# Output projection of a hybrid encoder layer: token tiles fetched at the same place, scaled, cast and split five pieces later

## The chip, the cores and the metric

The kernel runs on one core of a Trainium2 chip. The metric is the device time of one execution in microseconds (us), and the time of a kernel is the median of its runs. Engines are named as in the profile: PE is the matrix engine and PEld its weight loads, DVE the vector engine, ACT the scalar engine, POOL the GpSimd engine, and SP the engine whose queue (SPq) issues the DMAs. "PEclk" is the clock that PE was granted, as a share of full speed.

## What is computed

One encoder layer over 2048 tokens of width 1024, in float32. Two mixers run on one input projection, a chunked state-space mixer (SSD) and an RWKV-7 mixer, each bidirectional and 512 wide; an output projection, a residual with layer norm, and an MLP follow.

```
y_ssd = ssd_bidir(z, xbc, dt_raw, ...)                  # (2048, 512), RMS-normed in two groups, times norm_g
y_rwkv = rwkv7_bidir(rw, mu_rwkv, ...)                  # (2048, 512)
mix = concatenate([y_ssd, y_rwkv], -1) @ w_out          # the output projection, (2048, 1024)
h = layer_norm(ALPHA * h + mix, ln1_g, ln1_b)
h = layer_norm(ALPHA * h + square(relu(h @ w_fc)) @ w_proj, ln2_g, ln2_b)
```

## The kernel before

The program has three stages. `phase_in` makes the input projection and starts the SSD; `phase_rwkv` runs the RWKV recurrence and, in its gaps, what is left of the SSD and then the output projection; `phase_mlp` takes up what remains of the output projection and runs the MLP. In the profile the recurrence runs from about 1060 to 1970 us.

**The recurrence.** `phase_rwkv` walks over 32 units `u` (16 chunks of tokens, two groups of heads). A unit has four generators that `weave` interleaves: `chain(u)`, the serial part, whose state passes through `zt` (L1182), `zv` (L1185) and PE's products `ch` (L1150); `prep(u + 3)`, which loads `rk`, `bk0` and `E` (L997 to L1001) and makes the operands `bk` (L1007), `kr` (L1009, L1024), `at` (L1025) and `ra` (L1026); `inverse(u + 2)`, which inverts 16x16 blocks on POOL in 15 steps of two instructions, `ltmp` and `ln` (L1065, L1066); and `merge(u + 1)`, which makes the 64x64 inverses of it. The inverse is reached through DRAM: `prep` writes `at` to `ad` (L1050), `inverse` reads it back as `la` (L1056), writes its result to `nd` (L1069) and reads that as `ni` (L1072). All these DMAs are issued by SP, one behind the other.

**The output projection.** `out_pieces` is a generator that is drawn on by `dense` at set points of `chain` and `merge`, eight pieces in a unit. A piece (`DENSE`) is three matmuls of 128x512; `HELD` ends a draw without work. Its first pass goes over the 16 token tiles with the SSD half of `w_out` (`products(ops, True)`: two halves of 512 columns, 12 matmuls each), the second pass with the RWKV half, from unit 19 on (`FA`), and ends in the layer norm.

**A token tile.** `load` (L813) fetches `h`, the residual (L815), `yr`, the mixer's output, in two DMAs (L818), and in the first pass `rsb`, the rows of RMS factors (L821). It then scales `yr` in four DVE instructions (L823), casts it to `yh` on ACT (L825) and takes the rest `yl` on POOL (L827). It is called one tile ahead, before the pieces of the tile in hand. The pool `part_w` has two buffers of each name, so the `yr` of tile j + 2 cannot be fetched before the `yl` of tile j has been taken.

**What sets the order.** The order in the code is the order of priority; a scheduler with a timeline of its own then places the instructions on each engine. On the chip an engine takes its instructions in that fixed order, and a waiting one holds all behind it.

Of the kernel before, what the change touches and what calls it, by code (L numbers as in the profile page):

```python
# [19 lines left out]
NT = T // P  # L20
# [182 lines left out]
def ppc(k, name, j):  # L203
    c = _PP[name] + j
    return k.pp[:, c:c + 1]
# [576 lines left out]
DENSE, HELD, LAST, END = "dense", "held", "last", object()  # L782


def out_pieces(k):
# [3 lines left out]
    with ExitStack() as ctx:  # L789
# [3 lines left out]
        def weights(c0):  # L793
            wh, wl = [cp.tile([P, 4, D], F32R, name=n) for n in ("woh", "wol")]

            def raw(i):
                w = wk.tile([P, 4, P], F32, name="yr").rearrange("p a t -> p (a t)")
                r = (c0 + i // 2) * P
                nc.sync.dma_start(w, I["w_out"][r:r + P, 512 * (i % 2):512 * (i % 2) + 512])
                return w  # L800

            w = raw(0)
            yield
            for i in range(8):
                nxt = raw(i + 1) if i < 7 else None
                cs = wh[:, i // 2, 512 * (i % 2):512 * (i % 2) + 512], wl[:, i // 2, 512 * (i % 2):512 * (i % 2) + 512]
                nc.scalar.copy(cs[0], w)
                nc.gpsimd.tensor_tensor(cs[1], w, cs[0], ALU.subtract)
                w = nxt
                yield  # L810
            k.wo = wh, wl

        def load(t, ys, first):  # L813
            h = wk.tile([P, D], F32, name="h")
            nc.sync.dma_start(h, k.hD[t])  # L815
            yr = wk.tile([P, 4, P], F32, name="yr")
            for g in range(2):
                nc.sync.dma_start(yr[:, 2 * g:2 * g + 2], ys[g][:, :, P * t:P * t + P].rearrange("a p t -> p a t"))  # L818
            if first:
                rsb = wk.tile([P, 2, P], F32, name="rsb")  # L820
                nc.sync.dma_start(rsb, rsD[:, t].unsqueeze(0).broadcast_to([P, 2, P]))  # L821
                for c in range(4):
                    nc.vector.scalar_tensor_tensor(yr[:, c], yr[:, c], ppc(k, "ng", c), rsb[:, c // 2], ALU.mult, ALU.mult)  # L823
            yh = wk.tile([P, 4, P], F32R, name="yh")
            nc.scalar.copy(yh, yr)  # L825
            yl = wk.tile([P, 4, P], F32R, name="yl")
            nc.gpsimd.tensor_tensor(yl, yr, yh, ALU.subtract)  # L827
            return t, h, yh, yl

        def products(ops, first, rows=None):  # L830
            (wh, wl), (t, h, yh, yl) = k.wo, ops
            for hf in range(2):
                hs = slice(512 * hf, 512 * hf + 512)
                pt = k.psg.tile([P, 512], F32, name=k.psg_name)
                mm = [(yh, wh), (yh, wl), (yl, wh)]
                mm = [(y[:, c], w[:, c, hs]) for c in range(4) for y, w in mm]
                for i, (y, w) in enumerate(mm):
                    nc.tensor.matmul(pt, y, w, start=(i == 0), stop=(i == 11))
                    if i == 11:
                        if first:  # L840
                            nc.vector.scalar_tensor_tensor(h[:, hs], h[:, hs], ALPHA, pt, ALU.mult, ALU.add)
                        else:
                            nc.vector.tensor_tensor(h[:, hs], h[:, hs], pt, ALU.add)
                    if i + 1 in (CUTS[2 * (t % 2) + hf] if first else (3, 6, 9, 12)):
                        yield DENSE
            if rows:
                ln_apply(k, wk, h, *rows, k.eps[:, 0:1], True)
            nc.sync.dma_start(k.hD[t], h)
# [42 lines left out]
        nc.sync.dma_start(rsD.rearrange("g c t -> (g c) t"), rt)  # L891
        yield
        order = [t for s in range(NT // 2, NT) for t in (NT - 1 - s, s)]
        ops = load(order[0], k.yS, True)
        for j in range(NT):
            nxt = load(order[j + 1], k.yS, True) if j + 1 < NT else None
            yield
            yield from products(ops, True)
            ops = nxt
        ws = weights(4)  # L900
        next(ws)
        for p in gates((0, 3)):
# [4 lines left out]
        rows = []  # L907
# [8 lines left out]
        nxt = None  # L916
        ready = lambda j: j < NT and k.final[order[j]] == 2
        for j in range(NT):
            while not ready(j):
                yield HELD  # L920
            if nxt:
                ops = nxt
            else:
                ops = load(order[j], k.yR, False)
                for _ in range(HL):
                    yield HELD
            while k.u < FA + j // FB:
                yield HELD
            nxt = load(order[j + 1], k.yR, False) if ready(j + 1) else None
            yield  # L930
            yield from products(ops, False, rows)
            k.finals = j + 1
            yield LAST


def phase_rwkv(k):
    nc, tc, I = k.nc, k.tc, k.I
    with ExitStack() as ctx:
# [321 lines left out]
        def weave(main, others):  # L1260
# [10 lines left out]
            for o in others:  # L1271
                if o[0] is not k.ssd:
                    while step(o[0], o[5]) is not END:
                        pass

        k.fill = out_pieces(k)
        k.credit = 0.0
        k.final = [0] * NT
# [23 lines left out]
def ln_apply(k, pool, x, g, b, eps, spread=False):  # L1302

    nc = k.nc
    mean, rs = ln_stats(k, pool, x, eps)
    if spread:
        sh = pool.tile([P, 1], F32, name="ln_sh")
        nc.vector.scalar_tensor_tensor(sh, mean, -1.0, rs, ALU.mult, ALU.mult)
        nc.scalar.activation(x, x, AF.Identity, scale=rs, bias=sh)
    for row, mul in ((g, True), (b, False)):  # L1310
        c = 0
        for r in row:
            cs = slice(c, c + r.shape[1])
            c = cs.stop
            if spread:
                nc.gpsimd.tensor_tensor(x[:, cs], x[:, cs], r, ALU.mult if mul else ALU.add)  # L1316
            elif mul:
                nc.vector.scalar_tensor_tensor(x[:, cs], x[:, cs], mean, r, ALU.subtract, ALU.mult)
            else:
                nc.vector.scalar_tensor_tensor(x[:, cs], x[:, cs], rs, r, ALU.mult, ALU.add)  # L1320
# [364 lines left out]
```

## Time and profile before

| | |
|---|---|
| median of 3 runs | 3360.61 us (3358.46 to 3367.17) |
| the profiled execution's own time | 3365.71 us |
| its span, first to last instruction | 3363.9 us |
| PE busy over the span | 2999.4 us (89%) |
| DVE, ACT, POOL busy | 2166.7, 1535.1, 1584.2 us |
| mean granted clock of PE | 0.92 |
| scaling of `yr` (L823) | x64, median 351 ns, 1147.5 to 1463.7 us |
| cast to `yh` (L825) | x32, median 618 ns |
| rest `yl` (L827) | x32, median 1280 ns |

A row of the timeline has the start, the length, the engine, the line, what is written from what, and how many instructions are merged into the row; in brackets how long the engine had been idle before it and what ended that. A row of windows has, for one stretch of time, the busy time of PE, PEld, DVE, ACT and POOL, the granted clock, the share of the DMA engines and the GB/s. A row of waits has the engine and line that waited, for what, the total, the number of times and the longest.

### The profile page before, as it was taken

What the parts mean: (1) busy time and instruction counts of PE and PEld (TensorE: products, weight loads), DVE (VectorE), ACT (ScalarE), POOL (GpSimd) and SP (SyncE); (2) the same over time, 40 slices, a digit from 0 to 9 for tenths busy, and PEclk for the clock granted to TensorE, in tenths of its full rate; (3) what the DMA queues carried; (4) which work ended last, traced back from release to release, by engine and by line L of the source; (5) the groups of instructions that cost most, each with busy time, mean ns of one, the idle gap of its engine ahead of it and who ended that gap; (6) DMA issues with size and microseconds to landing.
All of it is one profiled execution on the core that took longest, in us unless ns stands there. A gap on an engine that the chain in (4) does not pass through costs nothing. (4 is left out here: it accounts for less than half of the span.)

```text
span 3363.9 us, 63959 instructions
## 1 busy us (share of the span) xinstructions
PE 2999.4 (89%) x23783; PEld 2394.6 (71%) x23783; DVE 2166.7 (64%) x3671; ACT 1535.1 (46%) x2993; POOL 1584.2 (47%) x1972
## 2 busy tenths in 40 slices
PE   5979999988887799898898886999899989999997
PEld 3767877766675577676666664888787868887886
DVE  7798556667666455554577658767877744466446
ACT  3556323333334445455565544544544553344333
POOL 0352124444445333334466665555566335555645
PEclk9989999889886688897798887999999989999998
DMA  6445355776778666666666554777799475566554
GB/s 209 135 157 185 120 148 176 199 214 195 201 205 251 150 165 161 155 167 163 170 181 174 142 155 152 234 252 234 258 323 314 141 297 190 198 213 212 189 197 153
DMA packets 728183, 650.23 MB, mean 193 GB/s; under 512 B 204064, under 2 KB 578496, under 8 KB 727232
## 3 DMA queue, kind: packets, MB, share of 16 engines
q1 hardware_dynamic: 727872, 646.15, 62.5%
q8 instruction: 187, 3.06, 0.4%
q14 instruction: 124, 1.02, 0.1%
HBM read 403.43 MB, written 242.57 MB: 192 GB/s over the span
## 5 line engine op out<-in xcount | busy, mean ns | idle before, releaser
L1553 DVE TENSOR_TENSOR ul<-ul,uh 128x1024 fp32r<-128x1024 f32 x112 | 241.3, 2156 | 293.9 <-ACT uh L1552 293.6
L1553 POOL TENSOR_TENSOR pl<-pl,ph 128x1024 fp32r<-128x1024 f32 x112 | 287.9, 2575 | 277.9 <-ACT ph L1552 277.8
L1507 PE MATMUL ps<-hh,wh 128*128 128x512 f32 x896 | 352.2, 394 | 19.8 <-ACT wh L1370 6.6
L266 PE MATMUL psg<-hh,wh 128*128 128x512 f32 x864 | 357.2, 414 | 7.3 <-ACT u L285 6.6
L1611 PE MATMUL ps<-ph,uh 128*128 128x512 f32 x896 | 349.0, 392 | 10.4 <-ACT ph L1552 8.7
L1611 PE MATMUL ps<-pl,uh 128*128 128x512 f32 x896 | 351.6, 393 | 5.0 <-POOL pl L1553 5.0
L267 PE MATMUL psg<-hh,wl 128*128 128x512 f32 x864 | 354.5, 410 | 0.0
L268 PE MATMUL psg<-hl,wh 128*128 128x512 f32 x864 | 353.2, 410 | 1.4 <-DVE hl L236 1.4
L1507 PE MATMUL ps<-hl,wh 128*128 128x512 f32 x896 | 350.6, 392 | 1.5 <-DVE hl L1430 1.4
L1507 PE MATMUL ps<-hh,wl 128*128 128x512 f32 x896 | 351.0, 392 | 0.9 <-DVE wl L1371 0.9
L1611 PE MATMUL ps<-ph,ul 128*128 128x512 f32 x896 | 350.4, 392 | 0.0
L1371 DVE TENSOR_TENSOR wl<-wa,wh 128x512 fp32r<-128x512 f32 x217 | 209.5, 970 | 88.9 <-ACT wh L1370 87.9
L1065 POOL TENSOR_TENSOR ltmp<-ln,la 128x30 f32<-128x30 f32 (+10 forms) x480 | 123.6, 258 | 255.7 <-DMA la<-ad 225.6
L1552 ACT CAST ph<-pl 128x1024 fp32r<-128x1024 f32 x112 | 117.7, 1051 | 274.2 <-DMA pl<-pD 274.2
L1370 ACT CAST wh<-wa 128x512 fp32r<-128x512 f32 x217 | 133.0, 618 | 207.2 <-POOL wa L1343 100.2
L1507 PEld LDWEIGHTS ps<-hh,wh 128*128 128x128 f32 x896 | 169.8, 190 | 59.2 <-ACT wh L1370 7.9
L266 PEld LDWEIGHTS psg<-hh,wh 128*128 128x128 f32 x864 | 169.6, 196 | 47.4 <-ACT u L285 8.1
L1611 PEld LDWEIGHTS ps<-ph,uh 128*128 128x128 f32 x896 | 169.4, 189 | 47.0 <-ACT ph L1552 9.5
L1611 PEld LDWEIGHTS ps<-pl,uh 128*128 128x128 f32 x896 | 169.8, 190 | 43.9 <-POOL pl L1553 8.7
L268 PEld LDWEIGHTS psg<-hl,wh 128*128 128x128 f32 x864 | 168.4, 195 | 39.7 <-issue 3.4
L1507 PEld LDWEIGHTS ps<-hl,wh 128*128 128x128 f32 x896 | 169.5, 189 | 37.5 <-DVE hl L1430 1.8
L267 PEld LDWEIGHTS psg<-hh,wl 128*128 128x128 f32 x864 | 169.7, 196 | 36.3 <-issue 2.6
(322 smaller groups left out, 7087.6 us busy)
## 6 DMA issues: line engine op xcount, KB each, us to landing
uD<-ua SPq DMA_DIRECT2D x224, 256.0 KB, 2.9
ul<-uD SPq DMA_DIRECT2D x112, 512.0 KB, 4.6
pl<-pD SPq DMA_DIRECT2D x112, 512.0 KB, 3.7
wa<-in_w_fc_dram SPq DMA_DIRECT2D x124, 256.0 KB, 3.4
pD<-sc SPq DMA_DIRECT2D x112, 256.0 KB, 4.2
rk<-rk SPq DMA_DIRECT2D x64, 384.0 KB, 4.7
h<-hD SPq DMA_DIRECT2D x48, 512.0 KB, 4.0
eD<-et SPq DMA_DIRECT2D x32, 514.0 KB, 2.7
```

The source lines that it names most:

```text
L266: nc.tensor.matmul(pt, wh[:, c], hh[:, c], start=(c == 0), stop=False)
L267: nc.tensor.matmul(pt, wl[:, c], hh[:, c], start=False, stop=False)
L268: k.lag = nc.tensor.matmul(pt, wh[:, c], hl[:, c], start=False, stop=(c == KC - 1))
L1065: eng.tensor_tensor(tv, ln[:, 0:m, r:r + 1].broadcast_to([P, m, w]), la[:, r:r + 1, r + 1:16].broadcast_to([P, m, w]), ALU.mult)
L1370: nc.scalar.copy(hi, x)
L1371: nc.vector.tensor_tensor(lo, x, hi, ALU.subtract)
L1507: nc.tensor.matmul(pt, x, y, start=(n == 0 and i not in (2, 3)), stop=(n == 11 and i not in (1, 5)), skip_group_check=True)
L1552: nc.scalar.copy(hi, x)
L1553: eng.tensor_tensor(lo, x, hi, ALU.subtract)
L1611: nc.tensor.matmul(banks[j], x, z, start=(g == 0 and s == 0), stop=(g == NG - 1 and s == 5))
```

## The change

`load` is cut in two. `fetch` issues the DMAs of a tile and stands where `load` stood; `prepare` scales, casts and splits the tile. A new generator `after` passes the pieces of `products` on and calls `prepare` for the next tile once the sixth piece (number 5, counted from 0) has been made. For the very first tile `prepare` comes after four `HELD`, with one more behind it. In the second pass a tile that could not be fetched ahead is prepared after the `HL` draws that it already waited for.

```
-        def load(t, ys, first):
+        def fetch(t, ys, first):
             h = wk.tile([P, D], F32, name="h")
             nc.sync.dma_start(h, k.hD[t])
             yr = wk.tile([P, 4, P], F32, name="yr")
...
             if first:
                 rsb = wk.tile([P, 2, P], F32, name="rsb")
                 nc.sync.dma_start(rsb, rsD[:, t].unsqueeze(0).broadcast_to([P, 2, P]))
+                return t, h, yr, rsb
+            return t, h, yr, None
+
+        def prepare(raw):
+
+            t, h, yr, rsb = raw
+            if rsb is not None:
                 for c in range(4):
                     nc.vector.scalar_tensor_tensor(yr[:, c], yr[:, c], ppc(k, "ng", c), rsb[:, c // 2], ALU.mult, ALU.mult)
             yh = wk.tile([P, 4, P], F32R, name="yh")
...
-        ops = load(order[0], k.yS, True)
+        def after(pieces, raw, n=5):
+
+            ops = None
+            for i, p in enumerate(pieces):
+                if p is DENSE:
+                    if i == n and raw:
+                        ops = prepare(raw)
+                    yield p
+            return ops
+
+        raw = fetch(order[0], k.yS, True)
+        for _ in range(4):
+            yield HELD
+        ops = prepare(raw)
+        yield HELD
         for j in range(NT):
-            nxt = load(order[j + 1], k.yS, True) if j + 1 < NT else None
+            raw = fetch(order[j + 1], k.yS, True) if j + 1 < NT else None
             yield
-            yield from products(ops, True)
-            ops = nxt
+            ops = yield from after(products(ops, True), raw)
...
-                ops = load(order[j], k.yR, False)
+                raw = fetch(order[j], k.yR, False)
                 for _ in range(HL):
                     yield HELD
+                ops = prepare(raw)
             while k.u < FA + j // FB:
                 yield HELD
-            nxt = load(order[j + 1], k.yR, False) if ready(j + 1) else None
+            raw = fetch(order[j + 1], k.yR, False) if ready(j + 1) else None
             yield
-            yield from products(ops, False, rows)
+            nxt = yield from after(products(ops, False, rows), raw)
```

No instruction is added or taken away; the order on the engines changes from about 1147 us to the start of the MLP. Lines behind L821 have higher numbers in the changed kernel: L1182 (`zt`) becomes L1203, L1024 (`kr`) L1045, L827 (`yl`) L834, L1069 (`nd`) L1090.

On DVE, at the end of a unit of the first pass, before (`n` is a step of `merge`, `zt` and `zv` the state of the chain, `bk`, `kr` and `ra` operands of `prep`):

```order
L1024 TENSOR_TENSOR kr<-ps,rc 64x4x64 x2
L1097 STREAM_TRANSPOSE n_12093<-dd 128x256
L823 SCALAR_TENSOR_TENSOR yr<-yr,pp,rsb 128x128 x4
L1182 TENSOR_TENSOR zt<-zz_11640,ch 128x256
L1185 TENSOR_TENSOR zv<-zt,dtab 64x4x64 x2
L1186 TENSOR_TENSOR zz_11850<-zt,dtab 128x256
L841 SCALAR_TENSOR_TENSOR h<-h,psg 128x512
L1026 TENSOR_TENSOR ra<-ps,rc 128x4x64 x2
L1007 TENSOR_TENSOR bk<-bk_12306,E 128x2x128 x2
L1024 TENSOR_TENSOR kr<-ps,rc 64x4x64 x2
```

The same place in the changed kernel:

```order
L1118 STREAM_TRANSPOSE n_12075<-dd 128x256
L848 SCALAR_TENSOR_TENSOR h<-h,psg 128x512
L1203 TENSOR_TENSOR zt<-zz_11621,ch 128x256
L1206 TENSOR_TENSOR zv<-zt,dtab 64x4x64 x2
L1207 TENSOR_TENSOR zz_11832<-zt,dtab 128x256
L1047 TENSOR_TENSOR ra<-ps,rc 128x4x64 x2
L1028 TENSOR_TENSOR bk<-bk_12288,E 128x2x128 x2
L830 SCALAR_TENSOR_TENSOR yr<-yr,pp,rsb 128x128 x4
L1045 TENSOR_TENSOR kr<-ps,rc 64x4x64 x2
L1047 TENSOR_TENSOR ra<-ps,rc 128x4x64 x2
L1190 COPY zv<-ch 64x4x64
```

The four scalings have moved from right ahead of `zt` to behind `zt`, `zv` and the first `bk` of the next unit, right ahead of `kr`.

On POOL, in one inverse of the first pass, before (steps of `ltmp` and `ln`; the inverse starts with the 128x15 one):

```order
L1065 TENSOR_TENSOR ltmp<-ln,la 128x15
L1066 TENSOR_TENSOR ln<-ln,ltmp 128x15
L1065 TENSOR_TENSOR ltmp<-ln,la 128x14
L1066 TENSOR_TENSOR ln<-ln,ltmp 128x14
L1065 TENSOR_TENSOR ltmp<-ln,la 128x26
L1066 TENSOR_TENSOR ln<-ln,ltmp 128x2x13
L827 TENSOR_TENSOR yl<-yr,yh 128x512
L1065 TENSOR_TENSOR ltmp<-ln,la 128x24
```

The same inverse in the changed kernel, near its end (128x8 is the last step):

```order
L1086 TENSOR_TENSOR ltmp<-ln,la 128x21
L1087 TENSOR_TENSOR ln<-ln,ltmp 128x7x3
L834 TENSOR_TENSOR yl<-yr,yh 128x512
L1086 TENSOR_TENSOR ltmp<-ln,la 128x14
L1087 TENSOR_TENSOR ln<-ln,ltmp 128x7x2
L1086 TENSOR_TENSOR ltmp<-ln,la 128x8
L1087 TENSOR_TENSOR ln<-ln,ltmp 128x8
```

The rest `yl` has moved from behind the third step to behind the thirteenth of fifteen.

On SP, from the store of a finished tile to the read of the next `la`, before:

```order
L848 DMA hD_90<-h 128x1024
L818 DMA yr<-yS_128 128x2x128
L818 DMA yr<-yS_129 128x2x128
L815 DMA h<-hD_91 128x1024
L821 DMA rsb<-rsD 128x2x128
L1069 DMA nd<-ln 512x1x16
L1203 DMA yaD_125<-ye 128x2x128 x2
L1069 DMA nd<-ln 512x1x16
L999 DMA bk_12306<-bk_106 128x4x128
L997 DMA rk<-rk_105 128x6x128
L1072 DMA ni<-nd 64x8x16 x2
L1050 DMA ad<-at 64x8x64 x2
```

The same stretch in the changed kernel:

```order
L855 DMA hD_90<-h 128x1024
L818 DMA yr<-yS_128 128x2x128
L818 DMA yr<-yS_129 128x2x128
L1090 DMA nd<-ln 512x1x16
L815 DMA h<-hD_91 128x1024
L1224 DMA yaD_125<-ye 128x2x128 x2
L1090 DMA nd<-ln 512x1x16
L1018 DMA rk<-rk_105 128x6x128
L1020 DMA bk_12288<-bk_106 128x4x128
L821 DMA rsb<-rsD 128x2x128
L1093 DMA ni<-nd 64x8x16
L1071 DMA ad<-at 64x8x64 x2
```

The fetches of `h` and `rsb` now stand between the writes of `nd` and the write of `ad`, and one of the two reads of `ni` stands behind `ad`. The units of the changed kernel take turns in threes: in the next one `yaD` and `h` stand ahead of both `nd`, and in the one after that both `ni` stand ahead of `ad`.

## The prediction

> **What bounds the kernel now.** The change moves instructions only while the recurrence runs with the first and second pass of the output projection in its gaps. The chain of what ended last does not reach back into that stage (it begins at 2377.91 us), so I read the stage from windows cut at `zt`, the chain's state, which comes once a unit. The first window holds eleven units of the first pass; the three after it are single units in which the scaling of a tile no longer stands on DVE ahead of `zt`, as all 16 tiles are scaled by 1463.7 us.
>
> ```profile
> 1182.16:1463.98 281.82, 256.93 (x4708) 199.19 (x4708) 158.99 (x397) 137.97 (x396) 97.59 (x345) 0.88 0.63 163
> 1463.98:1483.60 19.62, 18.65 (x379) 14.52 (x379) 13.19 (x33) 11.17 (x33) 2.98 (x12) 1.00 0.54 122
> 1483.60:1509.00 25.40, 22.47 (x434) 17.75 (x430) 14.22 (x32) 12.44 (x36) 9.47 (x33) 0.93 0.62 162
> 1509.00:1536.60 27.60, 23.92 (x434) 18.61 (x429) 14.22 (x33) 12.43 (x36) 9.45 (x33) 0.88 0.53 142
> ```
>
> A unit takes 281.82 / 11 = 25.62 us. Next I read who waits in the eleven units.
>
> ```profile
> POOL ltmp L1065 <- DMA la<-ad: 105.8, 11, 10.9
> ...
> DVE yr L823 <- DMA yr<-yS: 36.2, 11, 6.0
> ...
> PE ch L1150 <- DVE zt L1182: 22.7, 10, 4.0
> ```
>
> So DVE sits 36.2 us before the scalings, in eleven waits, with `zt` right behind them, and PE then waits 22.7 us for `zt`. That is the stall at which the change is aimed. But POOL waits longer, once a unit, for `la`. Whether the first stall costs anything is a question of which loop closes last, so I followed one unit through POOL and SP.
>
> ```profile
> 1251.37 0.21 POOL L1065 TENSOR_TENSOR ltmp<-ln,la 128x15 f32<-128x15 f32 x1 [9.43 <-DMA la<-ad]
> ...
> 1253.05 1.27 POOL L827 TENSOR_TENSOR yl<-yr,yh 128x512 fp32r<-128x512 f32 x1
> ...
> 1260.42 0.33 POOL L1066 TENSOR_TENSOR ln<-ln,ltmp 128x21 f32<-128x21 f32 x1
> ...
> 1261.97 0.21 POOL L1066 TENSOR_TENSOR ln<-ln,ltmp 128x8 f32<-128x8 f32 x1
> ...
> 1276.51 0.31 POOL L1065 TENSOR_TENSOR ltmp<-ln,la 128x15 f32<-128x15 f32 x1 [8.65 <-DMA la<-ad]
> ```
>
> The inverse starts at 1251.37 (I call this point P), ends at 1262.18, and the next one starts at 1276.51: 25.14 us from P to P. What lies between is SP's queue:
>
> ```profile
> 1254.35 0.87 SPq L818 DMA_DIRECT2D yr<-yS  x2
> 1256.82 0.33 SPq L815 DMA_DIRECT2D h<-hD  x1
> 1259.90 0.36 SPq L821 DMA_DIRECT2D rsb<-rsD  x1
> 1262.21 0.55 SPq L1069 DMA_DIRECT2D nd<-ln  x1
> 1262.85 1.09 SPq L1203 DMA_DIRECT2D yaD<-ye  x2
> ...
> 1267.51 1.29 SPq L1072 DMA_DIRECT2D ni<-nd  x2
> 1268.85 1.64 SPq L1050 DMA_DIRECT2D ad<-at  x2
> 1270.74 0.42 SPq L999 DMA_DIRECT2D bk<-bk  x1
> 1272.59 1.67 SPq L1056 DMA_DIRECT2D la<-ad  x2
> ```
>
> `nd` leaves 0.03 us after the inverse ends; `ad`, of the next inverse, stands behind `ni` and leaves the moment `ni` has been issued; `la` follows when `ad` has landed. **Loop one** is thus 10.84 (P to `nd`) + 6.64 (`nd` to `ad`) + 3.74 (`ad` to `la`) + 3.92 (`la` to P) = 25.14 us. No scaling is in it. The rows of DVE and ACT close **loop two**:
>
> ```profile
> 1258.64 1.23 DVE L823 SCALAR_TENSOR_TENSOR yr<-yr,pp,rsb 128x128 f32<-128x128 f32 x4 [5.93 <-DMA yr<-yS]
> 1259.80 0.41 DVE L1182 TENSOR_TENSOR zt<-zz,ch 128x256 f32<-128x256 f32 x1
> ...
> 1266.51 0.88 DVE L1024 TENSOR_TENSOR kr<-ps,rc 64x256 f32<-64x256 f32 x2 [3.04 <-PE ps L1019]
> ```
>
> ```profile
> 1266.97 0.87 ACT L1025 COPY at<-ps 64x256 f32<-64x256 f32 x2 [1.35 <-DVE kr L1024]
> ```
>
> `yl` ends at 1254.32, and 0.03 us later SP sends for `yr`, whose buffer it frees; the scaling starts 4.32 us after `yl` ended, then come `zt`, `kr` and `at`, which is ready at 1267.84. That is 16.47 us after P, and SP reaches `ad` only at 17.48. So loop two has 1.0 us of slack: the stall is real and almost free. The three single units say the same. The first, 19.62 us, shows the chain running ahead once; the next two take 25.40 and 27.60 us without any scaling, since another wait has come in:
>
> ```profile
> 1501.50 0.76 DVE L1009 TENSOR_TENSOR kr<-rk,E 128x256 f32<-128x256 f32 x2 [3.93 <-DMA rk<-rk]
> ```
>
> `rk` is fetched by the same SP queue.
>
> **The change part by part.** No instruction is new; the four scalings, the cast and the split cost what they cost. Three things move.
>
> (a) *DVE.* The scalings leave the place ahead of `zt` for the one ahead of `kr`. What is late next there is again their `yr`. `zt` came 8.43 us after P (1259.80 - 1251.37); without 1.16 us of scaling, and with about 3.7 us from `zt` to the end of the first `bk`, DVE reaches the scalings at about P + 10.9. Queued behind them are `kr`, `ra` and the copy of `zv` for which PE's next chain product waits.
>
> (b) *POOL.* `yl` goes from behind step 3 to behind step 13. Step 13 ended at 1260.75 with one `yl` already done, so `yl` now ends at P + 9.38 rather than P + 2.95, and `yr` is sent for 6.4 us later. With the same 4.32 us it lands at P + 13.7: **the wait does not go, it is 2.8 us in place of 5.93 and stands one step later.** The unknown here is the landing under the new neighbours on the queue; the profile's median for these DMAs is the nearest row:
>
> ```profile
> yr<-yS SPq DMA_DIRECT2D x22, 128.0 KB, 3.8
> ```
>
> I keep 4.32, which holds the issue of both DMAs, with 3.8 below it and the longest wait of the table, 6.0, above. Then loop two becomes 9.38 + 4.32 + 1.16 (scaling) + 1.33 (`kr` start to `at` end, 1266.51 to 1267.84) = 16.19 us from P to `at`, against 16.47 before: the same length. At the lower bound it is 15.7, at the upper 17.9, which is 0.4 over the 17.48 at which SP is ready.
>
> (c) *SP.* Between `nd` and `ad` the units take turns in threes. In the first kind `h` (0.33) and `rsb` (0.36) come in and one `ni` (half of 1.29) goes behind `ad`: +0.04. In the second kind `yaD` (1.09) and `h` go ahead of `nd` and are issued while POOL still works: -1.09 + 0.36 - 0.65 = -1.38. In the third, `h` and `rsb` come in: +0.69. The mean is -0.22 us a unit, 12 units: **-2.6 us**. The bounds are all units like the second kind (-16.6) and all like the third (+8.3). In the second kind SP reaches `ad` at 17.48 - 1.38 = P + 16.1 and `at` is ready at 16.19, so nothing more can be won there.
>
> (d) *PE* has its gap elsewhere: in mid-unit, at the product behind the copy of `zv`, not at the unit's start. After a gap PE is slow for long:
>
> ```profile
> 1207.99 0.80 PE L838 MATMUL psg<-woh,yh 128*128 128x512 f32 x1
> ...
> 1225.98 0.39 PE L838 MATMUL psg<-wol,yh 128*128 128x512 f32 x1
> ```
>
> ```profile
> 1208.20:1236.30 28.10, 28.10 (x429) 21.84 (x430) 14.91 (x37) 12.61 (x37) 11.11 (x40) 0.68 0.57 147
> ```
>
> The same matmul costs 0.80 us at 1207.99 and 0.39 us only 18 us later, and the unit behind it has PE busy for 28.10 of 28.10 us at a granted clock of 0.68, where the first single unit above had 18.65 of 19.62 at 1.00. So a slow unit is one that PE itself bounds; I take the number of such units as unchanged, and leave the other case to the rivals.
>
> One rule speaks against such a price. The Trainium skill, page "TensorE: Matmul & The Clock Gate", Part 1 (The HAM clock gate), says that half clock comes after an idle window of about 3.4 us and full clock after some 3.4 us of sustained work. By it the second rival below has no price: an estimate from that page is 1.7 us lost for each gap, far from filling a unit, and the forecast would stay as it is. The 18 us between the two matmuls do not agree with it, so the sum and the chances go by the rows.
>
> (e) *The second pass* keeps its tiles at the same units, and there the cast waits for `yr` on ACT:
>
> ```profile
> ACT yh L825 <- DMA yr<-yR: 11.0, 4, 6.5
> ```
>
> The order still has the first two casts side by side, so I take 0; the bounds are all of it gained and as much again lost, 11 us each way. The same row serves for the reordering between the two passes, which the trace of before cannot show.
>
> The sum is -2.6 us. The profiled execution took 3365.71 us (span 3363.9 and 1.8 around it), so it would become 3363.1; the runs' median lies 5.1 us below that execution, and the prediction is 3360.6 - 2.6 = 3358 us. As its own range the forecast has 3348 to 3370: the ends of (c) and (e) would not all fall on one side.
>
> **The rivals.**
>
> *The chain was the bound, and the stall cost time.* For it speaks the unit of 19.62 us, and that PE waits for `zt` ten times; against it the two units behind, at 25.40 and 27.60. If every unit went like the mean of these three, 24.21 us, eleven units would save 11 x (25.62 - 24.21) = 15.5 us: 3345 us. If all went like the first, 11 x 6.0 = 66 us: 3295, the far end. Chance 0.27.
>
> *PE cools in every unit (slower).* By the rows under (d) a mid-unit gap leaves PE slow for the two thirds of a unit that follow, the copy of `zv` and so `zt` come later, and PE itself becomes the bound, as in the unit shown under (d), 28.10 us. 11 x (28.10 - 25.62) = 27 us: 3388 us. It decides if the new gap reaches the 2.3 us (22.7 / 10) that PE now waits for `zt`, in each unit and not in every third or so. Against it: once a slow PE is late, the wait for `yr` is over before DVE comes to it, the gap closes, and the next unit is fast again. Chance 0.17.
>
> **How the numbers follow.** The forecast has 0.50, the first rival 0.27, the second 0.17, and 0.06 is left for shifts behind the first pass of which I know nothing. About 0.3%, 10 us, is what a measurement of this kernel can tell from no change. Faster than that (below 3350.5) are the first rival but for its mild end (0.25), the forecast's lower edge (0.06) and half the rest (0.03): 0.34. Slower (above 3370.7) are the second rival (0.17) and half the rest: 0.20. The other 0.46 is no change. The range of 8 in 10 is 3336 to 3384: it cuts off the first rival's far end (about 0.11) and what of the second lies above its price (about 0.08).
>
> **What would show it.** In the profile of the changed kernel: the wait of DVE for `yr<-yS` is still there, once a unit, at 2 to 4 us, and `kr` follows it instead of `zt`; the wait of PE for `zt` is gone and one for the copy of `zv` or for `kr` has come; `yr` is issued right after `yl`, late in the inverse; from one first `ltmp` to the next there are still about 25 us; the wait of POOL for `la` is still near 9 us a unit. If the first `ltmp` come 24 us apart or less, the first rival is right; if units at a clock near 0.7 stand one behind the other, the second. I am wrong altogether if the units from 1510 to 1970 us, and not those of the first pass, make the difference.

## The result and the profile after

The changed kernel takes 3406.26 us (median of 4 runs, 3399.89 to 3413.97); the kernel before, timed with it, 3361.27 us. The ratio is 1.0144, with a 95% interval of 1.0118 to 1.0170. The forecast was 3358 us with 3336 to 3384 as the range: the change costs 45 us where a gain of 3 was expected.

The profiled execution has a span of 3412.2 us, 48.3 more than before. Cut at the first `ltmp` of the inverses (point P of the prediction) and at the first product of the MLP, the two executions compare so:

| stretch | before | after | difference |
|---|---|---|---|
| start to P of unit 4 | 1170.5 | 1169.8 | -0.7 |
| P of unit 4 to P of unit 19 (first pass) | 391.6 | 412.2 | +20.6 |
| P of unit 19 to the MLP (second pass and tail) | 499.5 | 526.8 | +27.3 |
| the MLP | 1302.3 | 1303.4 | +1.1 |

So there are two losses, one in each pass. These are the windows of eleven units of the first pass (P of unit 5 to P of unit 16), the kernel before first; columns as in the prediction.

```profile
1199.74:1482.86 283.12, 258.22 (x4714) 199.96 (x4713) 159.51 (x398) 139.51 (x400) 99.45 (x352) 0.89 0.63 161
```

```profile
1199.80:1503.30 303.50, 254.44 (x4744) 195.88 (x4745) 160.00 (x400) 138.43 (x398) 99.54 (x353) 0.87 0.60 150
```

The work is the same on every engine and the clock nearly so (0.89 and 0.87); a unit takes 303.50 / 11 = 27.59 us in place of 25.74. It is time in which all engines wait. Who waits, in the same window after:

```profile
DVE yr L830 <- DMA yr<-yS: 79.2, 14, 9.1
...
PE ps L1054 <- ACT bkt L1056: 49.1, 11, 6.3
...
POOL ltmp L1086 <- DMA la<-ad: 123.8, 12, 15.6
```

DVE's wait for `yr`, the one at which the change is aimed, has more than doubled (36.2 us before, in eleven units). PE's wait for `zt` is gone, and one in mid-unit has come. All this looks as if the late scalings were the cost. One unit, followed through ACT and SP, says otherwise (P = 1310.26, an inverse of the second kind):

```profile
1323.90 0.36 ACT L1046 COPY at<-ps 64x256 f32<-64x256 f32 x1 [6.42 <-DVE kr L1045]
1324.56 0.37 ACT L1046 COPY at<-ps 64x256 f32<-64x256 f32 x1
```

```profile
1319.97 0.87 SPq L818 DMA_DIRECT2D yr<-yS  x2
1320.94 0.41 SPq L1224 DMA_DIRECT2D yaD<-ye  x1
1321.45 0.41 SPq L815 DMA_DIRECT2D h<-hD  x1
1321.95 0.40 SPq L1224 DMA_DIRECT2D yaD<-ye  x1
1322.45 1.29 SPq L1090 DMA_DIRECT2D nd<-ln  x2
...
1326.59 0.45 SPq L821 DMA_DIRECT2D rsb<-rsD  x1
1327.66 0.62 SPq L1093 DMA_DIRECT2D ni<-nd  x1
1328.37 1.27 SPq L1071 DMA_DIRECT2D ad<-at  x2
...
1333.34 1.32 SPq L1077 DMA_DIRECT2D la<-ad  x2
```

`at` is ready at 1324.93, although the scalings waited, and `ad` leaves only at 1328.37: loop two has 3.4 us of slack. So it is in every one of the eleven units: each half of `at` is ready some 2.9 us or more before the `ad` that stores it leaves. What closes last is SP's loop: wherever the trace has the landings (some are missing), `ni` leaves within 0.1 us of the landing of the second `nd`, `ad` right behind `ni`, and `la` within 0.1 us of the landing of `ad`. This loop has grown. Averaged over the eleven units, from P to `nd` 11.47 us (before 11.09), `nd` to `ad` 6.83 (5.98), `ad` to `la` 4.93 (4.29), `la` to P 4.36 (4.38). `yaD` and `h` stand ahead of `nd` here, but behind `yr`, which SP may send only when `yl` is done, at 1319.95; so `nd` leaves 1.2 us after the inverse has ended (1321.29).

The last view is that of the DMAs in the same windows: how often, how large, and the median time from issue to landing. Before, then after:

```profile
h<-hD SPq DMA_DIRECT2D x11, 512.0 KB, 3.7
...
ad<-at SPq DMA_DIRECT2D x22, 128.0 KB, 2.9
...
nd<-ln SPq DMA_DIRECT2D x22, 32.0 KB, 2.2
```

```profile
h<-hD SPq DMA_DIRECT2D x11, 512.0 KB, 4.7
...
ad<-at SPq DMA_DIRECT2D x22, 128.0 KB, 4.6
...
rsb<-rsD SPq DMA_DIRECT2D x9, 128.0 KB, 5.8
nd<-ln SPq DMA_DIRECT2D x22, 32.0 KB, 4.1
```

`nd` takes 1.9 us longer to land in the median, and `ad` 1.7. Both are on the loop: `ni` waits for `nd`, `ad` stands behind `ni`, and `la` waits for `ad`. The medians overstate it, though, since some landings are short and some long within one kernel: by the mean of the landings in the trace `nd` goes from 2.7 to 3.7 us and `ad` from 3.3 to 4.4.

### The profile page after: what moved, and what is told of

Its sections match the earlier page's. It is cut to its first block, busy times and chain, and to the rows that moved or that the text cites. A ratio compares the mean times of both kernels' runs of the same rounds, so it can differ in the third digit from the quotient of the medians.

```text
span 3412.2 us, 63949 instructions
## 1 busy us (share of the span) xinstructions
PE 2988.8 (88%) x23783; PEld 2380.2 (70%) x23783; DVE 2163.8 (63%) x3671; ACT 1534.6 (45%) x2993; POOL 1585.4 (46%) x1972
## 3 DMA queue, kind: packets, MB, share of 16 engines
q14 instruction: 124, 1.02, 0.1%
```

## The experiments

In the table "unit" is the mean of the eleven units from P of unit 5 to P of unit 16, and "second" the stretch from P of unit 19 to the MLP, both from one profiled execution; before they are 25.74 and 499.5, after 27.59 and 526.8. Each ratio is to the kernel before as it was timed beside that run. Two executions of one order differ by 0.3 us in the unit (before and its twin, run 1; after and its twin, run 2) and by up to 7 us in the second stretch (after and run 2), so the unit has grown by 1.2 to 1.9 us. The median landings differ too: `nd` 2.2 and 3.0 us in before and its twin, 4.1 and 3.8 in after and its twin; `ad` 2.9 and 2.8, 4.6 and 4.1. So the change adds 0.8 to 1.9 us to the one and 1.2 to 1.8 to the other.

| run | time, us | ratio to before (95%) | unit | second |
|---|---|---|---|---|
| 1 late, no `HELD` | 3360.7 | 1.0002 (0.998 to 1.0024) | 26.07 | 499.1 |
| 2 `HELD`, not late | 3413.4 | 1.0159 (1.0119 to 1.02) | 27.29 | 519.8 |
| 3 second pass shifted | 3366.1 | 1.0035 (1.0013 to 1.0057) | 25.83 | 509.9 |
| 4 `h`, `rsb` from ACT | 3395.0 | 1.0104 (1.007 to 1.0139) | 26.58 | 519.7 |
| 5 `h` from ACT, one `rsb` | 3367.8 | 1.0022 (1.0 to 1.0044) | 24.86 | 521.2 |
| 6 shift of two | 3388.7 | 1.0079 (1.005 to 1.0109) | 27.16 | 502.7 |
| 7 shift of seven | 3364.1 | 1.0006 (0.9986 to 1.0027) | 25.43 | 509.6 |
| 8 before, `yaD` from ACT | 3374.8 | 1.0031 (1.0012 to 1.0049) | 26.09 | 518.2 |
| 9 changed, `ad` from ACT | 3386.5 | 1.0066 (1.0044 to 1.0087) | 27.45 | 497.5 |
| 10 before, `ad` from ACT | 3413.0 | 1.0157 (1.0118 to 1.0196) | 27.89 | 520.5 |
| 11 shift of seven, `ad` from ACT | 3416.9 | 1.0169 (1.0119 to 1.0218) | 28.51 | 509.1 |
| 12 changed, one `rsb` | 3399.0 | 1.0117 (1.0086 to 1.0147) | 27.25 | 520.8 |
| 13 before, one `rsb` | 3355.5 | 0.9981 (0.9962 to 1.0) | 25.22 | 498.9 |
| 14 changed, one more `HELD` between | 3391.6 | 1.0102 (1.007 to 1.0133) | 27.53 | 506.9 |
| 15 shift of seven, one between | 3353.7 | 0.9987 (0.9966 to 1.0008) | 25.66 | 491.8 |

**What the change is (runs 1 and 2).** The diff does two things: it prepares a tile five pieces later, and it puts five `HELD` ahead of the first pass, by which all pieces come five draws later. Each was undone by itself.

```
-        raw = fetch(order[0], k.yS, True)
-        for _ in range(4):
-            yield HELD
-        ops = prepare(raw)
-        yield HELD
+        ops = prepare(fetch(order[0], k.yS, True))
```

> The changed kernel without its five HELD at the start of the first pass: the tile is still prepared after the sixth piece. In the built program the instructions then stand in the same order as before the change, on all five engines. If the time hangs on the order of the instructions (both theories below): 3361 us, within 0.3% of before. If late preparation by itself costs something that the order does not show (which buffer a tile gets, what a semaphore counts): 3375 to 3406.

Measured: 3360.7 us, no change from before. The program's order on all five engines is that of before: with the tile prepared five pieces later in the code, the scheduler puts the scalings, the cast and the split where they were, since it places them by when their data and buffers are ready on its timeline. Then the `HELD` alone, in the kernel before:

```
         ops = load(order[0], k.yS, True)
+        for _ in range(5):
+            yield HELD
```

> The kernel before, with only five HELD added ahead of the first pass; load is not cut in two. Its order is that of the changed kernel but for one pair of scalings at the very start. If the shift of the pieces by five draws is the whole change: 3406 us, 1.4% slower than before. If late preparation has a part in it: between 3361 and 3395.

Measured: 3413.4 us, as the changed kernel. So late preparation does nothing; **the whole effect is that of the five draws**, which shift the pieces against the units.

**Is the second pass a loss of its own? (run 3).** The same five `HELD`, but ahead of `ws = weights(4)`, between the passes.

> The kernel before, with the five HELD between the two passes: the first pass keeps its order, and the pieces behind it are shifted. Theory A (the lag of the first pass, 20 to 25 us, and that of the second, about as much, have separate causes): the units up to 1510 us as before, and 3375 to 3390 in all. Theory B (the second pass only hands on and enlarges what the first pass lost): 3361, within 0.3%.

Measured: 3366.1 us, which is in neither range; the first pass as before (25.83), the second stretch 509.9, the time 0.35% above before. A shift costs there by itself, as theory A has it, but 10 us in place of the 20 to 27 us of the changed kernel.

**SP's queue or DVE's wait? (runs 4, 5, 12, 13).** In the changed kernel `h` and `rsb` were taken off SP's queue.

```
-            nc.sync.dma_start(h, k.hD[t])
+            nc.scalar.dma_start(h, k.hD[t])
...
-                nc.sync.dma_start(rsb, rsD[:, t].unsqueeze(0).broadcast_to([P, 2, P]))
+                nc.scalar.dma_start(rsb, rsD[:, t].unsqueeze(0).broadcast_to([P, 2, P]))
```

> The changed kernel with the fetches of h and rsb issued from ACT's queue instead of SP's; the scalings stand and wait where they do in the changed kernel. Theory Q (SP's queue: h and rsb stand between nd and ad, and their landing slows nd and ad): from nd to ad about 5.5 us in place of 6.8, the first ltmp 26 us apart in place of 27.4, some 15 us won in the first pass, 3390. Theory W (the wait of DVE for yr ahead of kr, 79 us in place of 36, is the cost): no change, 3406. If the landing itself is the cost, whoever issues it: no change either, but from ad to la still 4.9 us.

Measured: 3395.0 us, a unit of 26.58. From `nd` to `ad` 4.48 us (6.83 in the changed kernel), but from `ad` to `la` 6.44 (4.93): more than half of what was won ahead of `ad` was lost again in its landing. The DMAs of this run:

```profile
h<-hD ACTq DMA_DIRECT2D x11, 512.0 KB, 3.3
...
ad<-at SPq DMA_DIRECT2D x22, 128.0 KB, 6.5
...
rsb<-rsD ACTq DMA_DIRECT2D x9, 128.0 KB, 6.0
nd<-ln SPq DMA_DIRECT2D x22, 32.0 KB, 2.2
```

ACT sends `h` early, and `nd` lands in 2.2 us again, as before. But it sends `rsb` right behind the scalings, and `ad`, on another queue, lands in 6.5. The Trainium skill, page "DMA: Bandwidth & Descriptors", section "Issuing engines are not separate DMA queues", says that DMAs of all issuing engines run on the same 16 DMA engines and interleave; the row of `ad` agrees, 6.5 us with `rsb` sent from the other queue. Next `rsb` was taken away too: it is fetched for the first tile, and all others are scaled by that one.

```
-                rsb = wk.tile([P, 2, P], F32, name="rsb")
-                nc.sync.dma_start(rsb, ...)
-                return t, h, yr, rsb
+                if t == order[0]:
+                    k.rsb1 = wk.tile([P, 2, P], F32, name="rsb")
+                    nc.sync.dma_start(k.rsb1, ...)
+                return t, h, yr, k.rsb1
```

> The kernel of the last run (h on ACT's queue), and rsb fetched for the first tile alone; all later tiles are scaled by that one, so the factors of the other tiles are left out. The four scalings and their wait for yr stay. In the last run the way from nd to ad fell to 4.48 us, but from ad to la rose to 6.44. Theory R (the fetch of rsb, 256 KB, is in flight beside ad and slows its landing): from ad to la 4.3 to 4.8 us, a unit of 25 to 25.5 us, some 12 to 18 us less than the last run, 3378 to 3383. Theory Y (what is left comes from the late yr, or from DVE's wait ahead of kr): from ad to la above 6, no change, 3395.

Measured: 3367.8 us; the unit fell to 24.86, below that of before, with `ad` to `la` at 3.92. Here the landings are short again (`rsb` has 128 KB by its row above, not the 256 of the expectation), while DVE still waits more than before for the late `yr`:

```profile
ad<-at SPq DMA_DIRECT2D x22, 128.0 KB, 2.9
...
nd<-ln SPq DMA_DIRECT2D x22, 32.0 KB, 2.4
```

```profile
DVE yr L831 <- DMA yr<-yS: 52.8, 16, 7.8
```

`yl` ends as late here as in the changed kernel (P + 9.5 to 10.2), and the unit is short. That speaks against the late `yr` and DVE's wait for it, though the wait fell too, from 79.2 us; the stronger evidence is that `at` was ready 2.9 us or more ahead of `ad` in the changed kernel. Two more runs take `rsb` alone away, from the changed kernel and from the kernel before.

> The changed kernel with rsb fetched for the first tile alone (the factors of the other tiles are left out); h, yr, the scalings and DVE's wait stay where they are. Theory R (the fetch of rsb between nd and ad lengthens the unit): a unit of 25 to 25.5 us in place of 27.6, and 3370 to 3380, what is left being the second pass. Theory H (h on SP's queue between the two nd, which the run with h on ACT's queue also took away, or yr's late fetch): 27 us or more, 3395 to 3406.

> The same taken from the kernel before, where rsb goes out ahead of nd: its order differs from that of before by the missing fetches alone. Theory R in its narrow form (rsb costs only where it stands between nd and ad): 25.5 us a unit, 3355 to 3363. If the DMA load of rsb costs wherever it stands: as much less as the changed kernel gains, 3330 to 3340, and rsb's place explains nothing.

Measured: 3399.0 us and 27.25 a unit in the changed kernel, so `rsb` by itself is not it, and theory R fell as it was put. Theory H named two causes, `h` and the late `yr`; run 5 has the late `yr` and a short unit, so `h` is left. In the kernel before it was 3355.5 and 25.22, as the narrow form of R had it. The DMAs of the changed kernel with one `rsb`, `h` still on SP between the two `nd`:

```profile
h<-hD SPq DMA_DIRECT2D x11, 512.0 KB, 4.4
...
ad<-at SPq DMA_DIRECT2D x22, 128.0 KB, 2.8
...
nd<-ln SPq DMA_DIRECT2D x22, 32.0 KB, 3.2
```

Now `ad` is fast and `nd` slow, the reverse of run 4. The median of 3.2 hides two kinds: in each of the eleven units the first `nd`, ahead of `h`, lands in 2.1 to 2.4 us, and the second, 1.6 us behind `h`, in 4.0 to 4.5. The two `yaD` also stand between them; in run 4, where they do so in five units and `h` has left long before, the second `nd` lands in 2.1 us in three of them, 3.0 in a fourth (one is not in the trace). **`h` just ahead of `nd` slows `nd`, `rsb` just ahead of `ad` slows `ad`**, and with either one left in flight the unit stays at 26.6 to 27.3. (The order of run 12 is not only short of `rsb`: all its units have `h` between the two `nd`, where every third one of the changed kernel has it ahead of both.)

Taking both away wins 27.59 - 24.86 = 2.73 us a unit in the changed kernel, more than the 1.85 us by which the units had grown; taking `rsb` away in the kernel before wins 0.52. How much `h` from ACT would win in the kernel before was not run, so the price of each fetch by itself is not known. Nor is it shown what in a fetch makes it dear. In the last two of the eleven units `rsb` is another 128 KB, rows of `ln1_b`, and `ad` lands in 2.6 to 4.1 us behind it in the changed kernel, where it takes 3.3 to 5.5 in the nine others, so the bytes alone do not seem to be the price.

**Other shifts (runs 6 and 7).** As run 2, with two and seven `HELD`.

> The kernel before with two HELD ahead of the first pass. yl then stands behind the eighth step, the scalings still ahead of zt, and h and rsb ahead of nd on SP. Theory Q (SP's queue between nd and ad): a unit of the first pass as before, 25.7 us, and 3361 to 3370 with what the second pass adds. Theory W (DVE's wait decides; loop two of the prediction, 13.5 us from the end of yl to at, with yl now ending some 4 us later): at ready at P + 20 rather than 16.5, ad waits for it, a unit of about 28 us and 3390.

Measured: 3388.7 us, 27.16 a unit, theory W's size (`yl` stands behind the seventh step in the trace). `h` and `rsb` stand ahead of `nd` here and yet the unit is long. Theory W's mechanism can be seen in a unit with P = 1278.85, where ACT and SP have

```profile
1296.89 0.37 ACT L1027 COPY at<-ps 64x256 f32<-64x256 f32 x1
```

```profile
1294.20 1.30 SPq L1074 DMA_DIRECT2D ni<-nd  x2
1295.70 2.17 SPq L1052 DMA_DIRECT2D ad<-at  x2
```

`at` ends at 1297.26, P + 18.4, and the second `ad` cannot go before. So loop two can bind when `yl` comes three us later and the scalings still stand ahead of `zt`. But it holds `ad` back by more than 0.1 us in only two of the eleven units, this one and another, and these last 26.7 and 25.2 us: not the long ones. In the others `ad` stands behind `ni`, and `ni` waits for `nd`, which lands slowly, in 4.1 us in the median:

```profile
ad<-at SPq DMA_DIRECT2D x22, 128.0 KB, 3.0
...
nd<-ln SPq DMA_DIRECT2D x22, 32.0 KB, 4.1
```

From `yr` to `nd` the order on SP is that of before, the distance in time is not: with `yl` three us later, `yr`, `h` and `rsb` all go out later, and `rsb` leaves 0.5 to 1.3 us ahead of the first `nd`, where it was 1.8 to 4.3 us before. So this run too shows the landing, of `nd` behind `rsb`, and theory W's number came near by luck. The kernel before has such units as well: the two in which `nd` took 3.6 us or more are its longest, 27.6 and 27.7 us.

> The kernel before with seven HELD ahead of the first pass. yl then stands behind the last step, and h and both yr are fetched behind ad; rsb goes ahead of nd. Theory Q: nothing of a tile stands between nd and ad, from nd to ad 5.5 us or less, a unit of 25 to 26 us, 3355 to 3370. If any shift costs, by the pieces' new places among PE's products: a unit of 27 us as in the changed kernel, 3400.

Measured: 3364.1 us, 25.43 a unit, as theory Q had it: a shift is not dear by itself. Here `h` and `yr` go out behind `ad` (but for one `yr` of the first unit), `rsb` some 10 us ahead of `nd`, and no other fetch of a tile leaves between `nd` and `ad`; only the store of a finished tile does. The landings are not short, though: `ad` takes 4.4 us in the median, and `ad` to `la` 5.06, as in the changed kernel. What makes up for it is that `yl` now stands behind the last step: `nd` leaves at P + 9.99 in place of 11.09.

**Is loop one a sum of issue times? (run 8).** The kernel before, with the two `yaD` issued by ACT (`nc.scalar.dma_start` at L1203).

> The kernel before with the two stores yaD issued from ACT's queue. It is to show whether loop one (P to nd to ad to la to P) sets the unit. If it does: from nd to ad about 1 us less (5.0), a unit of 24.7 us, and about 25 us less in all, 3335. If another loop sets the unit: the gap turns up elsewhere in the unit, 25.7 us, 3360.

Measured: 3374.8 us, nothing won, `nd` to `ad` 6.09 us. One unit of it:

```profile
1232.42 1.22 SPq L1069 DMA_DIRECT2D nd<-ln  x2
1233.74 0.57 SPq L999 DMA_DIRECT2D bk<-bk  x1
1235.18 1.29 SPq L1072 DMA_DIRECT2D ni<-nd  x2
1236.56 0.57 SPq L997 DMA_DIRECT2D rk<-rk  x1
1237.19 1.92 SPq L1050 DMA_DIRECT2D ad<-at  x2
```

Between `bk` and `ni` SP is idle for 0.9 us: `ni` waits for `nd` to land, and `ad` stands behind it. The issue time saved in front has become waiting; the loop is made of landings. The units swing from 24.4 to 29.5 us, and again by the landing of `nd`: the six units in which it took 3.4 us or more last 25.2 to 29.5 us, the five others 24.4 to 25.5. The 14 us lost fall in the second stretch (518.2 for 499.5), which was not followed.

**`ad` past the queue (runs 9 to 11).** `ad` is issued by ACT (`nc.scalar.dma_start` at L1050), in the changed kernel, in that before, and with seven `HELD`.

> The changed kernel with the two stores ad issued from ACT's queue, behind the copies at that they store. h, rsb and yr stay on SP's queue, and the scalings and DVE's wait where they were. Theory S (the path that sets the unit runs at, ad, la; ad waits in SP's queue behind whatever the shift puts ahead of it, in the first pass and in units 26 to 28 of the second): ad leaves at P + 15.5 to 16 in place of 18.3, a unit of the first pass of about 25 us, the second pass also shorter, 3350 to 3375. Theory C (what is in flight slows the landing of ad and nd, whoever issues them): the gain in the queue is given back from ad to la, as in the run with h and rsb on ACT's queue, 3390 to 3406.

> The kernel before with the two stores ad issued from ACT's queue. Theory S: ad leaves at P + 15.3 (the end of at) in place of 17.1, a unit of about 24 us in place of 25.7, and some 30 to 45 us less in all, 3315 to 3330. Theory C, or loop two behind it: a unit of 25 us or more, 3345 to 3365.

> Seven HELD ahead of the first pass, and ad issued from ACT's queue. With seven HELD at ended at P + 11 to 13, so ad could leave 2 to 3 us sooner than in the last run. Theory S: a unit of about 23 us, 3310 to 3330. Theory C: 25 us or more, 3355 to 3370.

Measured: 3386.5, 3413.0 and 3416.9 us. Theory S fell in all three, and theory C's range was missed by all three too. With `ad` elsewhere the scheduler laid the whole stage out anew: in the kernel before, one inverse now has no `yl`, the next has one behind the sixth step, the one after that two, and units of 35, 21 and 31 us follow one another, with `at` ready at P + 20 to 25 in the long ones. The edit changed much more than the queue of one DMA, so these runs say nothing clean about it. Run 9 is 20 us faster than the changed kernel, and by the second stretch (497.5 for 526.8), not by the unit (27.45).

**The second pass in step (runs 14 and 15).** The changed kernel with one more `HELD` between the passes, and seven ahead of the first pass with one between, eight in all, a unit's worth.

> The changed kernel with one more HELD between the two passes, by which DVE's order in the second pass is that of before in units 21 to 28 (SP's still differs in places). If the second pass of the changed kernel is slower by its order, which hangs on the phase of the pieces: from the inverse of unit 19 to the first product of the MLP about 500 to 510 us, as before (499), in place of 527, and 3380 to 3390 in all. If it is slower because the first pass ends later: 520 or more, 3400.

> The kernel before with seven HELD ahead of the first pass and one between the passes, eight in all, a whole unit. In the first pass h and yr go out behind ad and rsb ahead of nd; in the second pass DVE's order is that of before in units 22 to 28. If the time follows from what flies between nd and la in the first pass and from the phase in the second: 389 us from the inverse of unit 4 to that of unit 19 as with seven HELD (before 392), and some 500 from there to the MLP (before 499, with seven HELD 510): 3350 to 3360, no slower than before. If every new order costs: 3365 or more.

Measured: with one more `HELD` the first pass stays long (27.53) and the second stretch falls to 506.9; the time is 3391.6 us, a little above the range. The windows of that stretch, in the changed kernel and in run 14:

```profile
1582.00:2108.80 526.80, 421.92 (x6447) 317.81 (x6441) 331.19 (x636) 282.92 (x733) 308.12 (x606) 0.84 0.58 159
```

```profile
1579.00:2085.90 506.90, 409.77 (x6435) 309.40 (x6433) 339.24 (x636) 282.68 (x733) 303.86 (x606) 0.86 0.60 165
```

So most of the second loss hangs on the phase of the pieces, that is on their place against the units, not on the first pass ending late. The loss lies late in the stretch. From P of unit 19 to P of unit 26 the changed kernel takes 209.8 us (before 209.4), from there to P of unit 31 158.8 (143.0; in run 14 143.6), and from there to the MLP 158.2 (147.1). Run 15 came out at 3353.7 us, within its range, 0.9987 of before with an interval that holds 1: neither kernel is beaten with certainty, but a whole unit of shift, made of seven draws and one, costs nothing.

## Why the prediction was wrong

Two steps failed: (c) in the first pass, which lost 20.6 us, and (e) in the second, which lost 27.3.

- *That the stall is nearly free* was right, and so was the wait that does not go. `yl` was put at P + 9.38 and came at P + 9.7 in the unit shown; `at` was put at P + 16.2 and came at 14.7. Loop two did not come to bind in the changed kernel, and the unit of run 5 is shorter than before although DVE waits longer than before. The size of the wait, in (a) and (b), was off, without harm: 6.8 us in that unit for 2.8. `zt` came at P + 1.3, so DVE reached the scalings at P + 5.1 and not at P + 10.9, and `yr` landed sooner than was counted.
- **Step (c), SP's queue, failed**, on two counts. First, the gain of 1.38 us in the second kind rested on `yaD` and `h` being issued ahead of `nd` "while POOL still works". They stand behind `yr`, and `yr` waits for `yl`, which step (b) itself had put at the end of the inverse; nothing is left of POOL's work by then. In the unit shown `ad` left at P + 18.1, where 16.1 was forecast. Second, and larger, `h` and `rsb` were priced by their issue, 0.33 and 0.36 us, and the landings of what stands behind them were put at no change. Their price is that change: in the median 1.9 us more for `nd` and 1.7 more for `ad`. The loop grew by 0.85 us from `nd` to `ad`, 0.64 from `ad` to `la`, and 0.38 from P to `nd`. In place of -0.22 us a unit it is +1.85.
- *Loop one* was written as a sum of SP's steps. It fits the unit from which it was taken, but three of its four terms hold a landing, and run 8 shows that issue time saved between them is not won.
- *The first rival*, the chain as the bound, did not come: PE's wait for `zt` went and no unit of the eleven took less than 26.6 us.
- *The second rival*, PE cooling, had 3388 us and a wait in mid-unit, and a wait came there, 49.1 / 11 = 4.5 us a unit, if for `bkt` and not for the copy of `zv`. But the clock stayed (0.87 for 0.89, and 0.81 to 0.94 in each unit), and in no unit was PE busy for more than 91%. Its number was nearer for a wrong reason. Of the two matmuls shown under (d) the first opens a group of three and the second does not; like with like it is 0.63 us (1208.58) and 0.39. The granted clock bears the reading out: 0.50 from 1209 to 1225 us, with PE busy throughout.
- **Step (e) failed too, by size.** It took 0 for the second pass, within 11 us. It lost 20 to 27 us, more than half of the whole; run 14 gives back 20 of the 27 by one more draw. The wait on which (e) rests, the cast's for `yr`, did grow, from 11.0 us in four waits to 20.4 in five, but in run 14 it is 15.6 in four, and which wait makes the difference was not isolated: the cause stays open. The prediction's last sign, that it is wrong altogether if the units behind 1510 us make the difference, thus came true by half.
- What the change does was not seen: the rows of the order were read as the work of late preparation, but all of it came from the five `HELD` (runs 1 and 2).

## What to carry to other kernels

A DMA that is moved in an in-order queue is to be priced by what it does to the landing of the small transfers behind it, not by the fraction of a microsecond of its issue: look which loop runs through memory, and keep large fetches out of the stretch between its write and its read, and out of the microsecond or so ahead of the write. The order in the queue does not tell it; the distance in time does (run 6). Before a price is put on a move, see whether what stands ahead of it in the queue waits. And where a scheduler places the instructions, undo each line of a diff by itself and compare the orders: the line that names the change may do nothing.

## What the runs showed of the hardware

A write of 32 KB (`nd`) landed in 2.1 to 2.4 us ahead of a 512 KB fetch, and in 4.0 to 4.5 when it was issued 1.6 us behind it (run 12, the same units). One of 128 KB (`ad`) landed in 2.8 us in the median with no `rsb` ahead of it (run 12), in 4.6 and 4.1 behind that 128 KB fetch, which spreads its rows over all partitions, on the same queue (the changed kernel and run 2), and in 6.5 when the fetch came from ACT's queue (run 4): another queue was no shelter. In run 7 `ad` took 4.4 us with no `rsb` just ahead of it, so that fetch is not the only thing that slows it.

PE's granted clock stayed at 0.50 from 1209 to 1225 us of the kernel before, while PE was busy without a gap.
